# Head outputs of a 32-step linear recurrence with a token on each partition: row sums from the squaring instruction, scaling in the PSUM copy, four transposes back

## The chip, the core and the metric

The kernel runs on one core of one Trainium2 chip. The metric is the time of one execution in device microseconds (us); lower is better. Five engines matter: TensorE (PE in the profile; its weight loads are PEld), VectorE (DVE), ScalarE (ACT), GpSimd (POOL) and SyncE (SP), whose queue issues the weight transfers. Each engine takes its instructions strictly in the order in which they were written to its queue.

## The reference, cut to what matters

Two networks run one after the other on 512 tokens of width 1024. The change lies in the HGRN2 mixer near the end. It has 8 heads of 128 channels, works on chunks of 32 tokens, and normalizes each head's output for each token over the head's 128 channels:

```python
    o = o_intra + jnp.moveaxis(o_inter, 0, 2)
    o = o.transpose(0, 2, 3, 1, 4).reshape(B, S, H, DV)
    gate = jax.nn.silu(g_x.astype(jnp.float32)).reshape(B, S, H, DV)
    o = rms_norm(o, o_norm) * gate
    return o.reshape(B, S, HV).astype(h.dtype) @ w_o
```

where `rms_norm(x, g)` is `x * rsqrt(mean(x*x, axis=-1) + 1e-6) * g`.

## The kernel before

Activations lie channel-major: a tile of [128 channels, 512 tokens] for each block of 128 channels. Every large product runs as three products of parts (`mm3`: high by high, high by low, low by high), so an output block with 1024 inputs is 24 TensorE instructions of 128x512. A weight is loaded by SP into `raw`, its high part `wh` is made by ScalarE (line 140) and its low part `wl` by VectorE (line 123).

The mixer is the method `hgrn` (from line 1526). For head `hd` it runs `gates(hd + 1)` (two products, and the elementwise work on `A`, `Q`, `C`, `D`, `E`, `x` for the next head), `states(hd)` (the score products `sc`, the masked scores `hg_AT`, the turned keys `kv`/`kd`, the block states `st`), `out_gates(hd)` (the product whose gate is the tile `G`) and `outputs(hd)` (from line 1697), which is what changes. `vt` holds the values of all heads with a token on each partition. After the last head come the products with `w_o`: three output blocks (`mm`) that wait for the last heads' outputs, then blocks of half the tokens (`sm`).

The program's text isn't the order on the engines: a scheduler with its own model of times fixes, when the kernel is built, one order for each engine. So a changed instruction can move others. The order is fixed then, and an engine whose next instruction isn't ready stands still.

In PSUM, `hgrn` has two banks for `mm`, three for `sc`, one for `kv` and two for `po`. The tag `po` serves the head's output product and, before the change, two more tiles for each head: the sums over the channels (`tokstat`) and the factors spread over the partitions (`bcast`). Their products are these lines of the two helpers, and the factor itself is made by `rstd` (a small VectorE instruction at line 130 and a power on POOL at line 245):

```python
self.mm(ps[:, i * nb + tb : i * nb + tb + 1], a[:, s.start + tb * P : s.start + (tb + 1) * P], self.ones[:, 0:1])
...
self.mm(ps[:, o : o + P], c[:, tb : tb + 1].to_broadcast([P, P]), self.ident)
...
self.ts(out, sums, 1.0 / n, EPS)
self.pow_(out, out, -0.5)
```

In `outputs` before the change, the channels of the head lie on the partitions. ScalarE copies `po` (to the tile tagged `B`) and squares it (to `C`); TensorE sums the squares over the partitions (`po<-ones,C`), `rstd` gives `wo`, TensorE spreads it (`po<-ident,wo`), VectorE multiplies twice (line 133), and the result is split into `aH` (ScalarE) and `aL` (VectorE) for the products with `w_o`.

Of the kernel before, what the change touches and what calls it, by code (L numbers as in the profile page):

```python
# [20 lines left out]
P = 128  # L21
T = 512
# [26 lines left out]
class Acts:  # L49
    """Channel-major activations split exactly into two float32r parts."""  # L50
# [11 lines left out]
class Kern:  # L62
# [18 lines left out]
    def wpool(self, parts):  # L81
        """room for so many more split weights, taken in turns"""
        self.wx.append(ExitStack())
        pool = self.wx[-1].enter_context(self.pool(self.name("wp"), parts, side="left"))
        self.wslots.append([pool] * parts)

    def wclose(self):
        """takes back what was given last"""
        self.wx.pop().close()
        self.wslots.pop()  # L90
        self.wn = 0

    def psums(self, tags, keep=0):
        """PSUM banks, so many for each tag; the first pools may stay"""
# [16 lines left out]
    @contextmanager  # L111
    def ordered(self):
        """each engine issues the elementwise instructions within in the order of the program"""
        old, self.token = self.token, self.name("order")
        yield
        self.token = old
# [40 lines left out]
    def wload(self, src, k, m, eng=None):  # L157
        """src: DRAM [k*128, m] -> raw tile view [128, k, m]"""
# [31 lines left out]
    def gemm(self, w, col0, acts, K, evac, idx, m=P, leng=None, tag="mm"):  # L190
        """one chunk of m output channels: psum[m, T] = w[:, col0:col0+m].T @ acts"""
# [9 lines left out]
    def gemm_halves(self, w, cols, acts, K, evac, idxs, then=None, tags=None):  # L201
        """chunks of output channels, the first half of the tokens of all of them before the second"""
# [10 lines left out]
    def split(self, src, hi, lo, g=None):  # L213
        """hi + lo = src * g, exactly split; src fp32 in SBUF"""
# [8 lines left out]
    def tokstat(self, acc_list, s=FULL, tag="sm"):  # L223
        """acc tiles [128, T] -> psum [128 tok, len * blocks] of the sums over partitions"""
# [7 lines left out]
    def bcast(self, *cols, tag="sm"):  # L232
        """[128 tok, blocks] each -> psum [128, blocks * 128] each, the same on every partition"""
# [43 lines left out]
    def params(self, tag, rows_tile):  # L277
        """parameters, channel on partition: their loads and what turns them"""
# [22 lines left out]
    def block1(self):  # L301
# [10 lines left out]
        mod = self.cp.tile([P, 24], F32, tag="mod", name="mod")  # shift, 1 + scale, gate  # L312
# [6 lines left out]
        # what the output projection and its norm need again waits in DRAM  # L319
# [21 lines left out]
        def ada_load(pool, k, lo, n, bufs):  # L341
            """n blocks of w_ada, lo * 8 + k, (lo + 1) * 8 + k, .."""
# [6 lines left out]
        def ada_acc(acc, raw, steps=range(9)):  # L349
            """silu(c)'s products with them, but for the sum over partitions; two sums in turns"""  # L350
# [27 lines left out]
        # shift and scale of a chunk of channels are summed while the chunk before is modulated  # L378
        def modulated(k, xt, acc):
            """shift and scale, x turned and modulated"""  # L380
# [50 lines left out]
        def shift_evac(ps, mc, out, v3=False):  # L431
            """out = p + mu * (p one token before - p)"""
# [8 lines left out]
        # -------- masks  # L441
        mk2 = b([P, 2, RC], "mk2")  # columns t of A (s < t) and of R (s <= t); rows s twice
# [5 lines left out]
        # rows (head, s), columns (head, t): s in the lower, t in the upper half of one head  # L448
# [6 lines left out]
        # -------- B branch: low-rank inputs of decay and in-context rate  # L455
# [8 lines left out]
        hp = b_([P, 16], "hp")  # w0/2, a0/2, k_a/2, 1-k_a/2  # L464
# [22 lines left out]
        def prep(p):  # L487
            """what a pair of heads brings to the windows, in parts that other products may come between"""
# [52 lines left out]
        def lmat(p, hf):  # L541
            """for half of the windows of a pair: products of all of B | K with all of A | R, masked"""
# [14 lines left out]
        # -------- A branch: norm of v, mixing over the tokens of a block  # L557
# [56 lines left out]
        # -------- products that nothing waits for: they fill the tensor engine between the others  # L614
# [9 lines left out]
        def v_part(p):  # L624
            """values, and the bonus of the current token"""
# [5 lines left out]
        # gate of the B branch: (gn * g + b + bonus) * silu(gate) = gn * G2 + B2  # L631
# [43 lines left out]
        def fill(n):  # L675
            """so many steps of what fills"""
# [13 lines left out]
        def a_free():  # L690
            """the windows' products take the A branch's place"""
# [4 lines left out]
            # of the first four windows where the residual will be  # L696
# [45 lines left out]
        def inverse():  # L742
            """inverses of the 32x32 diagonal blocks of I - L, one block per partition"""
# [29 lines left out]
        def merge(c):  # L773
            """inverses of the 64x64 blocks, transposed"""
# [36 lines left out]
        def chain(c, between):  # L811
            """one window; what else there is comes between its dependent products"""
# [4 lines left out]
            # one accumulation group per bank: the first product alone clears it  # L817
# [38 lines left out]
        def post(tb):  # L856
            """group norm over a head's channels, bonus, gate"""
# [27 lines left out]
        def out_gate(k):  # L885
            """gate of the output, one chunk"""
# [39 lines left out]
        def between(c, late):  # L926
            """the next window's inputs, and the norm of what is complete"""
# [56 lines left out]
        # -------- output projection, residual, layer norm  # L984
# [10 lines left out]
        def o_evac(n, i, ps, s):  # L995
# [5 lines left out]
            else:  # L1001
                self.tt(a1, a1, y, ALU.add)
                sq = (s1, s2)[n % 2][:, HALVES[s.start == 0]]  # the half that holds no sums now
# [3 lines left out]
        # the weight stays for the second half of the tokens, some of it where the attention's inputs will be  # L1007
# [59 lines left out]
    # chunk k of acts = res * gain, split  # L1067
# [7 lines left out]
    def sumsq(self, acc, y, k, pool, s, tag="sq"):  # L1075
        """acc[:, s] += y ** 2, the first for k = 0"""
# [12 lines left out]
    def rstd(self, out, sums, n, fac=None):  # L1089
        """out = (sums / n * fac + EPS) ** -0.5 for [128 tok, NB] columns"""  # L1090
# [7 lines left out]
    def norms(self, m, s2, g, w, s, pre, r2=None):  # L1098
        """res += m * rms(m) * gain; with r2 the true m is m * r2 per token;
        pre: the next norm's acts, gain, sums of squares and a pool"""  # L1100
# [32 lines left out]
    def gemm_tail(self, w, acts, K, evac, norm, begun=()):  # L1133
        """eight chunks; the last four by halves of the tokens, norm(s) after each"""
# [17 lines left out]
    def mla(self):  # L1152
        nc, I, tc = self.nc, self.I, self.tc
        if True:
# [8 lines left out]
            # -------- the products start before the first norm's per-token factor is known  # L1163
# [8 lines left out]
            def c_evac(i, ps, s):  # L1172
# [4 lines left out]
                else:  # split when the factor per token is there  # L1177
# [6 lines left out]
            # rotary key: its columns twice, so that both halves of the partitions hold it  # L1184
# [9 lines left out]
            # -------- rotation tables: cos, and sin with the sign of the row's half  # L1194
# [50 lines left out]
            # the queries' factor enters with the scale of the scores  # L1245
# [27 lines left out]
            # -------- values, token-major  # L1273
# [17 lines left out]
            # -------- attention  # L1291
            oa = self.new_acts()

            def scores(q, qr, k, qb):
                """softmax of the query block's scores, [128 queries, keys]"""
# [48 lines left out]
            def project_q(hp, tags=("mm", "mm")):  # L1344
# [11 lines left out]
                # one head each: its upper parts on its half of the partitions, the lower ones on the other  # L1356
# [37 lines left out]
    def mixer_out(self, nm, w_o, o, gpost, gpre, begun=()):  # L1394
        """res += rms(o @ w_o); the MLP's normed input"""
# [130 lines left out]
    def hgrn(self):  # L1526
# [3 lines left out]
        with ExitStack() as ox:  # L1530
            oa = self.new_acts()
            with ExitStack() as mx:
# [164 lines left out]
                def outputs(hd, AT, st, E, G):  # L1697
                    hs = slice(hd * P, (hd + 1) * P)
                    po = self.ptl("po")
                    for tb in range(NB):  # L1700
                        s = slice(tb * P, (tb + 1) * P)
                        self.mm(po[:, s], vt[tb][:, hs], AT[:, tb, :], start=True, stop=(tb == 0))
                        if tb:
                            self.mm(po[:, s], st[:, tb, :], E[:, s], start=False, stop=True)
# [72 lines left out]
```

## Time and profile before

| | before |
|---|---|
| median of three runs | 1627.69 us (1627.19 to 1629.02) |
| span of the profiled execution | 1623.7 us |
| TensorE busy, share of the span | 1554.1 us, 96% |
| VectorE busy | 947.0 us, 58% |
| ScalarE busy | 704.4 us, 43% |
| POOL busy | 325.0 us, 20% |
| transfers, mean | 100 GB/s |

The span runs from the first to the last instruction of the profiled execution. No time of its own is given for that execution beside the span; the median of the runs lies 4.0 us above the span, and that is what lies around it. The mixer's heads run from about 1026 to 1221.5 us of the span.

### The profile page before, as it was taken

To read this page: it belongs to the slowest core of one execution; us is meant where nothing else is said; L and a number is where in the kernel's file an instruction comes from. 1 tells how busy PE (TensorE), PEld (TensorE's weight loads), DVE (VectorE), ACT (ScalarE), POOL (GpSimd) and SP (SyncE) were. 2 spreads that over 40 slices of the span, in tenths; PEclk is the share of its full clock that TensorE was granted. 3 is DMA by queue.
4 is the path that set the end of the run, shared out by engine and by line. 5 is a ranking of instruction groups with operands and counts; after the bars stand their busy time and mean duration, and the time that the engine had idled before them with its cause. 6 is when DMAs were issued, how large, how long until landed. Compare 5 with 4: busy or idle time off the path is not lost. (4 is left out here: it accounts for less than half of the span.)

```text
span 1623.7 us, 22045 instructions
## 1 busy us (share of the span) xinstructions
PE 1554.1 (96%) x8389; PEld 1317.7 (81%) x8389; DVE 947.0 (58%) x1651; ACT 704.4 (43%) x1217; POOL 325.0 (20%) x459
## 2 busy tenths in 40 slices
PE   5987979999999999999999999999999999999998
PEld 4766768889978899888888887888889988888886
DVE  7798595678667738233343456677754824343445
ACT  3533315655666645332232334666535523322331
POOL 4465631234310023000000032222313200000000
PEclk9998889999999999999999999999999999999999
DMA  9732445544123133333333232322213223231421
GB/s 290 219 96 82 75 130 144 176 139 112 52 69 91 33 111 90 93 92 102 91 93 102 80 102 66 103 66 66 71 47 105 91 79 115 64 120 65 120 88 52
DMA packets 272894, 161.70 MB, mean 100 GB/s; under 512 B 29465, under 2 KB 253316, under 8 KB 272788
## 3 DMA queue, kind: packets, MB, share of 16 engines
q1 hardware_dynamic: 271492, 157.33, 33.6%
q0 software_dynamic: 1152, 2.70, 0.5%
q8 instruction: 66, 1.08, 0.3%
q14 instruction: 40, 0.33, 0.1%
q10 hardware_dynamic: 144, 0.26, 0.1%
HBM read 147.42 MB, written 11.53 MB: 98 GB/s over the span
## 5 line engine op out<-in xcount | busy, mean ns | idle before, releaser
L123 DVE TENSOR_TENSOR wl<-raw,wh 128x1024 fp32r<-128x1024 f32 (+2 forms) x228 | 272.1, 1194 | 291.1 <-ACT wh L140 287.0
L140 ACT CAST wh<-raw 128x1024 fp32r<-128x1024 f32 (+3 forms) x244 | 242.6, 996 | 449.1 <-PE mm L143 354.2
L143 PE MATMUL mm<-bL,wh 128*128 128x512 f32 (+1 forms) x752 | 282.6, 378 | 1.0 <-DVE bL L133 1.0
L143 PE MATMUL mm<-bH,wl 128*128 128x512 f32 (+1 forms) x752 | 281.5, 377 | 0.0
L143 PE MATMUL mm<-bH,wh 128*128 128x512 f32 (+1 forms) x752 | 278.9, 378 | 0.1
L143 PE MATMUL mm<-aH,wh 128*128 128x512 f32 (+1 forms) x656 | 240.6, 369 | 11.2 <-DVE gt L133 7.0
L143 PE MATMUL mm<-aH,wl 128*128 128x512 f32 (+1 forms) x656 | 236.8, 362 | 1.5 <-DVE wl L123 1.5
L143 PE MATMUL mm<-aL,wh 128*128 128x512 f32 (+1 forms) x656 | 237.7, 363 | 0.0
L143 PEld LDWEIGHTS mm<-bL,wh 128*128 128x128 f32 x752 | 141.1, 188 | 29.0 <-DVE bL L133 1.8
L143 PEld LDWEIGHTS mm<-bH,wl 128*128 128x128 f32 x752 | 141.1, 188 | 27.4
L143 PEld LDWEIGHTS mm<-bH,wh 128*128 128x128 f32 x752 | 139.1, 188 | 28.4 <-ACT hg_vt L137 0.5
L143 PEld LDWEIGHTS mm<-aH,wh 128*128 128x128 f32 x656 | 125.1, 191 | 33.4 <-DVE gt L133 7.9
L143 PEld LDWEIGHTS mm<-aH,wl 128*128 128x128 f32 x656 | 125.1, 191 | 20.7 <-DVE wl L123 1.9
L143 PEld LDWEIGHTS mm<-aL,wh 128*128 128x128 f32 x656 | 125.5, 191 | 18.3 <-issue 0.7
L143 PE MATMUL mm<-wh,aH 128*128 128x512 f32 x288 | 113.5, 396 | 1.5 <-ACT aH L140 1.5
L143 PE MATMUL mm<-wh,aL 128*128 128x512 f32 x288 | 112.6, 393 | 0.0
L143 PE MATMUL mm<-wl,aH 128*128 128x512 f32 x288 | 112.5, 392 | 0.0
L140 ACT CAST aH<-t 128x512 fp32r<-128x512 f32 (+1 forms) x74 | 41.1, 564 | 75.7 <-DVE t L123 75.5
L123 POOL TENSOR_TENSOR mlpt<-mlpt,sq 128x256 f32<-128x256 f32 (+1 forms) x9 | 11.9, 1320 | 306.5 <-ACT sq L137 306.5
L245 POOL TENSOR_TENSOR mlpss<-mlpss,pwm 128x1 f32<-128x1 f32 x4 | 2.2, 547 | 321.8 <-DVE mlpss L128 321.8
L123 DVE TENSOR_TENSOR aL<-t,aH 128x512 fp32r<-128x512 f32 (+1 forms) x74 | 45.0, 617 | 36.2 <-ACT aH L140 36.2
L143 PEld LDWEIGHTS mm<-wh,aH 128*128 128x128 f32 x288 | 54.6, 190 | 12.8 <-ACT aH L140 1.9
(546 smaller groups left out, 2831.4 us busy)
## 6 DMA issues: line engine op xcount, KB each, us to landing
raw<-in_mlp_w_dram SPq DMA_DIRECT2D x128, 512.0 KB
raw<-in_hgrn_w_in_dram SPq DMA_DIRECT2D x32, 512.0 KB
raw<-in_w_in_dram SPq DMA_DIRECT2D x23, 512.0 KB
ada<-in_w_ada_dram SPq DMA_DIRECT2D x16, 512.0 KB
raw<-in_w_out_dram SPq DMA_DIRECT2D x10, 512.0 KB
raw<-in_w_ada_dram SPq DMA_DIRECT2D x8, 512.0 KB
raw<-in_mla_w_o_dram SPq DMA_DIRECT2D x8, 512.0 KB
raw<-in_hgrn_w_o_dram SPq DMA_DIRECT2D x8, 512.0 KB
```

Source lines behind the costliest of these rows:

```text
L123: self.st((eng or self.nc.vector).tensor_tensor(out=out, in0=a, in1=b, op=op))
L140: self.st(self.nc.scalar.copy(out=out, in_=in_))
L143: i = self.nc.tensor.matmul(out, l, r, start=start, stop=stop, **kw)
L245: self.nc.gpsimd.tensor_tensor(out=out, in0=a, in1=cst[: a.shape[0], :n], op=ALU.pow)
```

## The change

Both products of `outputs` have their operands swapped, so that `po` holds the 128 tokens of a block on the partitions and the head's channels along the free axis. A token's sum of squares is then a sum along a row, which each of four squaring instructions of ScalarE leaves in a column of `wo` through its accumulator. `rstd` works on those four columns. ScalarE copies `po` in four pieces, each scaled by its tokens' factor (one value for each partition), TensorE turns each piece back with a transpose (`pt`, from the same `po` banks), and VectorE multiplies the turned tile by the norm's gain (with the half of the gate folded into a new column `hon`, made once) and the gate in one instruction, in place in `G`. The rest of the diff takes out comments and docstrings.

```diff
@@ in hgrn
+                hon = vp.tile([P, 1], F32, tag="hon", name="hg_hon")
+                self.ts(hon, self.pc("on"), 0.5)
...
@@ in outputs
                     for tb in range(NB):
                         s = slice(tb * P, (tb + 1) * P)
-                        self.mm(po[:, s], vt[tb][:, hs], AT[:, tb, :], start=True, stop=(tb == 0))
+                        self.mm(po[:, s], AT[:, tb, :], vt[tb][:, hs], start=True, stop=(tb == 0))
                         if tb:
-                            self.mm(po[:, s], st[:, tb, :], E[:, s], start=False, stop=True)
+                            self.mm(po[:, s], E[:, s], st[:, tb, :], start=False, stop=True)
                     o = self.tl(mp, [P, T], "B")
-                    self.copy(o, po)
                     sq = self.tl(mp, [P, T], "C")
-                    self.act(sq, po, AF.Square)
-                    wo = self.tl(mp, [P, NB], "wo")
-                    self.rstd(wo, self.tokstat([sq], tag="po"), P)
-                    pr = self.bcast(wo, tag="po")
-                    self.stt(o, o, self.pc("on"), pr, ALU.mult, ALU.mult)
-                    self.stt(o, o, 0.5, G, ALU.mult, ALU.mult)
-                    self.split(o, oa[hd][0], oa[hd][1])
+                    wo = self.tl(mp, [P, 2, NB], "wo")
+                    for tb in range(NB):
+                        s = slice(tb * P, (tb + 1) * P)
+                        self.act(sq[:, s], po[:, s], AF.Square, accum=wo[:, 0, tb : tb + 1])
+                    self.rstd(wo[:, 1], wo[:, 0], P)
+                    pt = self.ptl("po")
+                    for tb in range(NB):
+                        s = slice(tb * P, (tb + 1) * P)
+                        self.act(o[:, s], po[:, s], AF.Copy, scale=wo[:, 1, tb : tb + 1])
+                        self.turn(pt[:, s], o[:, s])
+                    self.stt(G, pt, hon, G, ALU.mult, ALU.mult)
+                    self.split(G, oa[hd][0], oa[hd][1])
```

On TensorE, the order changes from the first head's output on, and is the same again from the first `sm` product after the last head. Between two products of 128x512 that belong to one output block, "..." stands for the others of it. First, TensorE where head 3's output (`po_10178` before, `po_10180` after) is done and head 4's scores (`sc`) begin, before the change:

```order
L143 MATMUL po_10178<-E_9877,st_10134 128x128
L143 MATMUL mm_10251<-bL_6257,wh_10247 128x512
...
L143 MATMUL sc_10313<-D_10078,A_10001 128x128 x4
L143 MATMUL sc_10318<-E_10083,x_10097 128x128
L143 MATMUL po_10191<-ones,C_10188 128x1 x4
L143 MATMUL sc_10318<-E_10083,x_10097 128x128 x3
L143 MATMUL sc_10323<-E_1718_10101,K_1719_10102 64x64 x4
L143 MATMUL mm_10355<-bH_6250,wh_10351 128x512
...
L143 MATMUL po_10198<-ident,wo_10190 128x128 x4
L143 MATMUL kv_10334<-ident,x_10097 128x128 x3
```

The same place after the change:

```order
L143 MATMUL po_10180<-st_10136,E_9879 128x128
L143 MATMUL mm_10253<-bH_6260,wl_10250 128x512
...
L143 MATMUL sc_10315<-D_10080,A_10003 128x128 x4
L143 MATMUL sc_10320<-E_10085,x_10099 128x128 x4
L143 MATMUL sc_10325<-E_1715_10103,K_1716_10104 64x64 x4
L143 MATMUL mm_10357<-bH_6250,wh_10353 128x512
...
L149 MATMUL po_10197<-ident,B_10188 128x128
L143 MATMUL mm_10357<-bL_6259,wh_10353 128x512
...
L149 MATMUL po_10197<-ident,B_10188 128x128 x2
```

Before, 14 products stand between the output and the scores, the sums come among the scores, and the spread factors after 23 of the next block's 24 products. After, 7 products stand ahead of the scores, and the transposes come after the 13th, 16th and 17th product of the next block, one, one and two at a time.

Second, TensorE at the last head's output (`po_10896` before, `po_10898` after), before the change:

```order
L143 MATMUL po_10896<-E_10701,st_10852 128x128
L143 MATMUL mm_11075<-aL_8950,wh_11071 128x512
...
L143 MATMUL mm_11075<-aH_8951,wl_11072 128x512
L143 MATMUL po_10909<-ones,C_10906 128x1 x4
L143 MATMUL mm_10931<-aH_8953,wh_10927 128x512
...
L143 MATMUL mm_11075<-aH_8953,wl_11072 128x512
L143 MATMUL po_10916<-ident,wo_10908 128x128 x4
L143 MATMUL sm_11128<-aH_8941,wh_11106 128x256
```

The same place after the change:

```order
L143 MATMUL po_10898<-st_10854,E_10703 128x128
L143 MATMUL mm_10933<-aH_8953,wh_10929 128x512
...
L143 MATMUL mm_11077<-aH_8953,wl_11074 128x512
L149 MATMUL po_10915<-ident,B_10906 128x128 x4
L143 MATMUL sm_11130<-aH_8941,wh_11108 128x256
```

Before, 5 products, the sums, 9 products (the three blocks' inputs from head 6, `aH_8953`) and the spreading stand between the last output and the first `sm` product. After, the 9 products and the transposes stand there, and the 5 products have gone ahead of the output.

Third, ScalarE around head 3's output (`A` is the next head's gate), before the change:

```order
L137 ACT_TABLE_LOAD
L137 ACTIVATE A_10207<-A_10207 128x512
L140 COPY B_10186<-po_10178 128x512
L137 ACTIVATE C_10188<-po_10178 128x512
L137 ACT_TABLE_LOAD
L137 ACTIVATE A_10207<-A_10207 128x512
```

The same place after the change (`C,wo` are the squares with their sums, `B<-po,wo` the scaled copies):

```order
L137 ACT_TABLE_LOAD
L137 ACTIVATE A_10209<-A_10209 128x512
L137 ACTIVATE C_10189,wo_10190<-po_10180 128x128 x4
L140 CAST wh_10624<-raw_10622 128x1024
L137 ACTIVATE Q_10246<-x_10278 128x512
L137 ACTIVATE B_10188<-po_10180,wo_10190 128x128 x4
L137 ACT_TABLE_LOAD
L137 ACTIVATE A_10209<-A_10209 128x512
```

The second table load and the second pass over `A` have moved from right behind the square of `po` to behind the scaled copies, which wait for POOL's power. The number of table loads is the same.

## Rows read from the trace of the kernel before

**Rows 1.** Windows: stretch, its length, each engine's busy time (instructions), granted clock, DMA.

```profile
1026.00:1221.50 195.50, 195.43 (x1106) 166.57 (x1105) 135.97 (x211) 111.15 (x164) 54.16 (x119) 1.00 0.23 65
1221.50:1260.00 38.50, 36.55 (x271) 34.43 (x270) 19.65 (x28) 20.60 (x41) 13.65 (x13) 1.00 0.38 112
```

**Rows 2.** Chain that ended last: start, duration, engine, tile, line, instructions.

```profile
1400.07 200.75 PE mm L143 x874
```

**Rows 3.** Timeline of TensorE after head 0's output: start, duration, what.

```profile
1061.34 1.05 PE L143 MATMUL sc<-D,A 128*128 128x128 f32 x8
...
1063.83 0.50 PE L143 MATMUL mm<-bH,wh 128*128 128x512 f32 x1
...
1064.40 0.95 PE L143 MATMUL po<-ones,C 128*128 128x1 f32 x8
1065.21 0.48 PE L143 MATMUL mm<-bH,wl 128*128 128x512 f32 x1
1065.53 0.39 PE L143 MATMUL mm<-bH,wh 128*128 128x512 f32 x1
...
1072.61 1.05 PE L143 MATMUL po<-ident,wo 128*128 128x128 f32 x8
1073.50 0.61 PE L143 MATMUL po<-hg_AT,hg_vt 128*128 128x128 f32 x4
```

**Rows 4.** Timeline of TensorE, head 0's three transposed key blocks.

```profile
1047.60 0.49 PE L1680 MATMUL kv<-ident,x 128*128 128x128 f32 x3
1047.92 0.61 PE L143 MATMUL po<-hg_AT,hg_vt 128*128 128x128 f32 x4
```

**Rows 5.** Timeline of ScalarE: a 128x128 instruction with its accumulator read.

```profile
474.73 0.46 ACT L137 ACTIVATE P<-sm,st,w 128x128 f32<-128x128 f32 x1
475.09 0.19 ACT L137 ACTIVATION_READ_ACCUMULATOR P<-sm,st,w 128x1 f32 x1
475.18 0.39 ACT L140 CAST wh<-raw 128x256 fp32r<-128x256 f32 x1
```

**Rows 6.** Groups by line and form, ScalarE: busy us, mean ns | idle before.

```profile
L137 ACT ACTIVATE S<-S,PC 128x128 f32<-128x128 f32 x24 | 8.8, 397 | 0.3
...
L140 ACT COPY PT<-pt 128x128 f32<-128x128 f32 x8 | 2.2, 270 | 0.3 <-PE pt L1317 0.2
```

**Rows 7.** Timelines of ScalarE, VectorE and POOL behind the last head's output.

```profile
1216.47 0.59 ACT L140 COPY B<-po 128x512 f32<-128x512 f32 x1 [13.17 <-PE po L143]
...
1218.70 0.16 DVE L130 TENSOR_SCALAR wo<-po 128x4 f32<-128x4 f32 x1
...
1219.01 1.01 POOL L245 TENSOR_TENSOR wo<-wo,pwm 128x4 f32<-128x4 f32 x1 [9.57 <-DVE wo L130]
```

**Rows 8.** Timelines of TensorE, VectorE and POOL after head 1's output.

```profile
1085.96 0.95 PE L143 MATMUL po<-ones,C 128*128 128x1 f32 x8
...
1090.23 0.15 DVE L130 TENSOR_SCALAR wo<-po 128x4 f32<-128x4 f32 x1
...
1090.47 1.39 POOL L245 TENSOR_TENSOR wo<-wo,pwm 128x4 f32<-128x4 f32 x1 [1.24 <-DVE wo L130]
```

**Rows 9.** Timeline of TensorE, from the last head's output on.

```profile
1215.99 0.39 PE L143 MATMUL po<-E,st 128*128 128x128 f32 x2
1216.13 0.47 PE L143 MATMUL mm<-aL,wh 128*128 128x512 f32 x1
...
1217.61 1.05 PE L143 MATMUL po<-ones,C 128*128 128x1 f32 x8
...
1220.69 1.05 PE L143 MATMUL po<-ident,wo 128*128 128x128 f32 x8
1221.50 0.36 PE L143 MATMUL sm<-aH,wh 128*128 128x256 f32 x1
```

**Rows 10.** Windows of 4 us from a pause of TensorE on (columns as in Rows 1).

```profile
116.00:120.00 4.00, 0.97 (x6) 0.97 (x8) 4.00 (x7) 1.15 (x2) 0.20 (x1) 0.84 0.06 18
120.00:124.00 4.00, 4.00 (x26) 3.50 (x25) 2.30 (x6) 0.00 (x0) 1.18 (x1) 0.73 0.49 185
```

## The prediction

> **What bounds the kernel now.** I read the windows first. Over the eight heads (1026 to 1221.5 us) TensorE is busy 195.43 of 195.50 us at the full granted clock, while VectorE has 135.97 and ScalarE 111.15 us of work there [rows 1]; per head that is 24.4 us of TensorE, 17.0 of VectorE, 13.9 of ScalarE. From there to 1260 us TensorE is idle for 2 us, and the chain that ended last is then TensorE alone: 874 instructions in 200.75 us, 0.23 us for a 128x512 product [rows 2]. So a microsecond of TensorE taken out of the heads comes off the end, as long as nothing makes TensorE wait instead. What the other engines gain or lose counts only through such waits.
>
> **TensorE, removed.** I take a block's cost as the time from its start to the next start, since ends overlap. The sums over partitions take 1064.40 to 1065.21, 0.81 us for a head; where they stand ahead of a large product, that product takes 0.32 us instead of 0.23, 0.09 more [rows 3]. Spreading the factors takes 1072.61 to 1073.50, 0.89 us [rows 3]. Both are eight instructions for four blocks: each float32 product is two passes, even the one with a single column.
>
> **TensorE, added.** Four transposes of 128x128. The row for this form is the turned keys: three in 0.32 us, one pass each, so four are 0.43 us [rows 4]. Where they stand ahead of a large product the 0.09 us come on top. By the order, the four stand together ahead of small blocks in heads 0, 1 and 6, ahead of a large product in heads 2 and 4, and in three pieces among large products in heads 3 and 5 (three times 0.09). The swapped products keep their number and shape, 128x128 by 128x128 either way, so I cost them at nothing, and no row gives a reason for another value.
>
> So heads 0 to 6 save 0.81 + 0.89 - 0.43 = 1.27 us in heads 1 and 6, 1.36 in head 0 (whose sums stood among large products), 1.18 in heads 2 and 4, 1.00 in heads 3 and 5: together 1.36 + 2.54 + 2.36 + 2.00 = 8.3 us.
>
> **ScalarE, VectorE, POOL.** A head loses a 512-wide copy and square and gains four 128-wide squares, four accumulator reads and four scaled copies. An instruction of that width with its read takes 474.73 to 475.18, 0.45 us [rows 5]; a copy of 128x128 out of PSUM takes 0.27 us, one with a scale from a tile 0.40 [rows 6]. That is 1.8 + 1.6 us in place of two at about 0.59 [rows 7], so some 16 us of ScalarE in a head of 23 us, still with room. VectorE loses one pass of 512. These hide under TensorE except where TensorE waits for the result.
>
> **Heads 0 to 6, does TensorE wait?** From the last product of an output to the transposes TensorE has this to do in head 3: 7 products (1.6 us), the scores (1061.34 to 1063.83, 2.5 us [rows 3]), 13 products (3.0 us), 7.1 us in all; in the others, by the same count in the order, 6.8 to 8.3. The chain it must cover: squares 1.8, the small VectorE instruction and POOL's power 0.3 + 1.0 to 1.4 [rows 7, 8], copies 1.6, about 5.2 us. That leaves 1.5 us or more, so I take no wait here. If the cover is gone, TensorE stands still with the next head's output products behind it in its queue.
>
> **The last head.** Here little work is left. Before, from the last output (1216.13) to the first `sm` product (1221.50) lie 5.4 us, nearly full of work [rows 9]. After, I put the new chain on the same clock. Squares start at 1216.47, where the copy of `po` starts now [rows 7]; four at 0.45 end at 1218.4. The small instruction follows 0.1 later, the power starts 0.3 after that (as 1218.70 and 1219.01 stand) and takes 1.0 [rows 7], to 1219.8. Four scaled copies at 0.40 end at 1221.4, the last transpose and the `sm` product follow at 1221.6. TensorE has only nine products to fill this with, 2.1 us, then it idles about 2.8 us. So the `sm` products start as late behind the last output as before, though 5 products (1.15 us) have gone ahead of that output. The last head therefore costs 1.15 + 0.1 = 1.25 us instead of saving any.
>
> Bounds for this term: the cheapest rows, 0.27 for each square and copy with free reads [rows 6], bring the end 1.2 us earlier; the dearest, 0.46 + 0.19 for a square with its read in full [rows 5], 0.46 for a copy and 1.39 for the power [rows 8], bring it 1.4 us later. I take the middle because the pair in rows 5 is the same pair of instructions at the same width.
>
> The Trainium skill, page "VectorE: DVE Perf Modes", section on the TRN2 errata, speaks against splitting like this: ScalarE pays a fixed latency with every instruction, and tiles of 512 or more are advised. Its formula for a PSUM source (172 cycles plus the width, at 1.2 GHz) gives 0.25 us at 128, an estimate that agrees with the 0.27 us of rows 6 for a plain copy but has no accumulator read; with it eight instructions are 2.0 us instead of 3.4, and the sum would come to 1619.3 us.
>
> **The sum.** -8.3 + 1.25 = -7.0 us: the span from 1623.7 to 1616.7, and with the 4.0 us around it, from a median of 1627.69 to 1620.7 us. A change of 0.2%, 3.3 us, is about what a measurement of this kernel tells from none.
>
> **Rivals.**
> *The last head loses nothing.* If squares and copies are as cheap as the cheapest rows and no head pays the 0.09 us of a switch, the heads give up to 7 x 1.36 = 9.5 us and the last head costs nothing: about 1618.2. For it speaks that a plain PSUM copy takes 0.27 us; against it, the accumulator's read has its own row.
>
> *The pause costs the clock.* In the window from 116 us TensorE was busy 0.97 of 4 us, and the granted clock was 0.84 there and 0.73 in the next [rows 10]; the level below full is 1.2 GHz instead of 2.4. That loss is 0.16 x 4 + 0.27 x 4 = 1.7 us. The new pause, 2.8 us, is a little shorter. If it does the same, the time is 1622.4. [...]
>
> *The chain is late in every head.* After head 1 the sums start at 1085.96, but the small VectorE instruction that reads them runs at 1090.23, 3.3 us after their end, since VectorE does other instructions ahead of it, and POOL's power then takes 1.39 [rows 8]. After the change this instruction again stands behind other work of VectorE, and ScalarE queues the next head's second table load and pass over the gate behind the scaled copies. With 3.3 us more the chain is about 8.5 us against a cover of 6.8 to 8.3, a wait of some 1 us in each of seven heads: 1620.7 + 7 = 1627.7, no change. From 1.5 us each it is slower by more than the measurement tells, around 1631. Against it: the chain has 1.5 us or more in hand in every head, and head 1's delay didn't make TensorE wait before.
>
> **How the numbers follow.** The forecast, 1620.7, has a chance of 0.50; the larger gain 0.14; the clock's loss 0.18; the late chain 0.18, of which no change 0.10 and slower 0.08. The first three are faster by over 0.2%: 0.82. The range goes from 1617.5, just below the larger gain, to 1625.5, which takes in the bounds of the last head, the clock and a wait of up to 0.7 us a head, and leaves out about 2 in 10. The forecast's own range is 1619.5 to 1622.1, from the bounds of the last head.
>
> **What would show it.** In the changed kernel the heads from 1026 us on should take about 8 us less, with 32 one-pass transposes and no `po<-ones` or `po<-ident,wo`. TensorE should have no wait for `B` in heads 0 to 6, and one of 2 to 3.5 us for the last head's `B`. ScalarE's squares with their reads should stand about 0.45 us apart. The prediction is wrong if TensorE waits for `B` or for the next scores in the middle heads, if ScalarE's small instructions take over 0.65 us, or if the granted clock falls below 1.00 behind the last head.

## The result and the profile after

| | before | after |
|---|---|---|
| median | 1627.44 us (1625.90 to 1629.02, 4 runs) | 1616.88 us (1615.60 to 1619.43, 4 runs) |
| ratio, 95% interval | | 0.9936 [0.9922, 0.9950] |
| span of the profiled execution | 1623.7 us | 1613.8 us (its own time 1615.6 us) |
| head 0's first output product to the first `sm` product | 173.58 us [rows 4, 9] | 163.94 us |

The change makes the kernel 0.64% faster, 10.6 us where I had forecast 7.0, and the median lies 0.6 us under the low end of my range. The page's first part for the changed kernel, each engine's busy time, share of the span and instructions:

```profile
span 1613.8 us, 21901 instructions
PE 1542.8 (96%) x8293; PEld 1305.5 (81%) x8293; DVE 939.0 (58%) x1644; ACT 713.3 (44%) x1297; POOL 329.5 (20%) x459
```

TensorE lost 96 instructions: 64 for the sums, 64 for the spread factors, and 32 transposes came. Windows of the changed kernel (columns as in [rows 1], which they answer):

```profile
1026.00:1213.00 187.00, 186.15 (x1020) 156.56 (x1019) 130.61 (x204) 120.24 (x245) 58.00 (x119) 1.00 0.25 70
1208.00:1212.00 4.00, 3.15 (x16) 2.11 (x15) 0.37 (x2) 2.06 (x12) 1.61 (x2) 1.00 0.10 30
1212.00:1216.00 4.00, 4.00 (x28) 3.69 (x28) 1.24 (x2) 1.26 (x2) 0.00 (x0) 1.00 0.28 101
```

In the heads TensorE is idle for 0.85 us in 187, at the full granted clock, and the second row says where: behind the last head's output. The clock is 1.00 there and in the window behind. TensorE's waits of the changed kernel from 1020 to 1240 us (what waits for what: us in total, times, longest):

```profile
PE po L149 <- ACT B L137: 0.9, 1, 0.9
PE mm L143 <- ACT hgms L137: 0.5, 1, 0.5
```

So no transpose of heads 0 to 6 waits; the one wait for `B` is the last head's. (The wait for `hgms`, in the norm behind the heads, stands in the kernel before as well, with the same 0.5 us.) Groups by line and form of the changed kernel, 1026 to 1214 us (columns as in [rows 6]):

```profile
L245 POOL TENSOR_TENSOR wo<-wo,pwm 128x4 f32<-128x4 f32 x8 | 10.2, 1275 | 55.2 <-DVE wo L130 55.2
L137 ACT ACTIVATE B<-po,wo 128x128 f32<-128x128 f32 x32 | 9.1, 367 | 5.4 <-POOL wo L245 5.4
L137 ACT ACTIVATE C<-po 128x128 f32<-128x128 f32 x32 | 8.4, 278 | 15.4 <-PE po L143 15.4
L137 ACT ACTIVATION_READ_ACCUMULATOR C<-po 128x1 f32 x32 | 6.6, 207 | 0.0
```

A square's mean is 0.28 us and a read's 0.21, but they overlap. The timeline of ScalarE behind the last head's output shows how far apart they stand (start, duration, what):

```profile
1207.77 0.28 ACT L137 ACTIVATE C<-po 128x128 f32<-128x128 f32 x1 [1.84 <-PE po L143]
1207.94 0.19 ACT L137 ACTIVATION_READ_ACCUMULATOR C<-po 128x1 f32 x1
1208.04 0.27 ACT L137 ACTIVATE C<-po 128x128 f32<-128x128 f32 x1
...
1210.23 1.14 ACT L137 ACTIVATE B<-po,wo 128x128 f32<-128x128 f32 x4 [1.32 <-POOL wo L245]
```

From square to square it is 0.27 and then 0.25 us, read included, and four scaled copies take 1.14, 0.29 each. [Rows 5] had given 0.45 and [rows 6] 0.40. TensorE at the same place, which answers to [rows 9]:

```profile
1207.35 0.39 PE L143 MATMUL po<-st,E 128*128 128x128 f32 x2
1207.49 0.94 PE L143 MATMUL mm<-aH,wh 128*128 128x512 f32 x3
...
1210.66 1.10 PE L149 MATMUL po<-ident,B 128*128 128x128 f32 x4 [0.85 <-ACT B L137]
1211.52 0.36 PE L143 MATMUL sm<-aH,wh 128*128 128x256 f32 x1
```

**Where the time came from.** From the first large product behind the last output to the first `sm` product it is 1207.49 to 1211.52, 4.03 us, against 1216.13 to 1221.50, 5.37 us [rows 9]. Five products, 1.15 us, have gone ahead of that output, so the last head gains 1.34 - 1.15 = 0.19 us. From head 0's output to that large product it was 168.21 us and is 159.91, with the five products more: heads 0 to 6 give 8.30 + 1.15 = 9.45 us, 1.35 each. Together 9.64; the span fell by 9.9, since the heads began 0.3 us sooner. Behind the first `sm` product nothing changed: from its start to the end of the span it is 402.2 us before and 402.3 after.

Granted clock and start of the heads differ from one execution to the next, by some us that have nothing to do with the change (in every run the same 5456 TensorE instructions stand ahead of head 0's output): in the runs below head 0's output stands anywhere from 1047.6 to 1054.4 us. So I compare the stretch from head 0's first output product to the first `sm` product (173.58 before, 163.94 after), in which the granted clock was 1.00 but for the pauses told of below, and give the medians beside it.

### The profile page after: what moved, and what is told of

The parts are those of the page before. It is cut to its first block, busy times and chain, and to the rows that moved or that the text cites. A ratio compares the mean times of both kernels' runs of the same rounds, so it can differ in the third digit from the quotient of the medians.

```text
span 1613.8 us, 21901 instructions
## 1 busy us (share of the span) xinstructions
PE 1542.8 (96%) x8293; PEld 1305.5 (81%) x8293; DVE 939.0 (58%) x1644; ACT 713.3 (44%) x1297; POOL 329.5 (20%) x459
```

## The experiments

My theory after the result: every head's two float32 blocks cost 0.89 us each on TensorE and the transposes 0.43, in whichever order; ScalarE's chain costs only where TensorE has nothing else, in the last head, and there it is shorter than I had it. Rivals: that the gain comes from something else than the two blocks (the swapped products, ScalarE's or VectorE's lighter work), and that the prediction's 1.25 us for the last head was right and the heads gave still more.

### The sums over partitions again

```diff
                     for tb in range(NB):
                         s = slice(tb * P, (tb + 1) * P)
+                        self.mm(pt[:, tb : tb + 1], sq[:, s], self.ones[:, 0:1])
+                    for tb in range(NB):
+                        s = slice(tb * P, (tb + 1) * P)
                         self.act(o[:, s], po[:, s], AF.Copy, scale=wo[:, 1, tb : tb + 1])
```

> The changed kernel, but TensorE again sums the squares of each head with four one-column products, into the bank that the transposes overwrite; the sums are thrown away. I compare the stretch from head 0's first output product to the first half-width product behind the last head: 173.6 us before, 163.9 after the change. Theory (the gain is TensorE work taken out of a full engine): the block costs 0.89 us a head, 8 heads give 7.1, so the stretch is 171.0 and the time about 1624. Rival (the gain comes from the shorter chain or from the new order, and TensorE's small blocks are hidden): the stretch stays at 164 to 165 and the time at 1617.

Measured: stretch 1054.39 to 1223.94, 169.55 us, 5.6 more than after; median 1623.97 us, ratio to before 0.9981 [0.9970, 0.9991]. That is nearer to the theory's 171.0 than to the rival's 164 to 165, and 1.5 short. TensorE behind the last output in this kernel:

```profile
1216.75 0.39 PE L143 MATMUL po<-st,E 128*128 128x128 f32 x2
...
1221.77 0.95 PE L143 MATMUL po<-ones,C 128*128 128x1 f32 x8
...
1223.35 0.49 PE L149 MATMUL po<-ident,B 128*128 128x128 f32 x3
```

From 1216.89 to 1221.77, 4.9 us, stand large products; TensorE has no wait here. The scheduler put 21 products between the last output and the sums, 25 in all behind that output, where the changed kernel has nine, and the changed kernel's wait is gone. What hiding that wait is worth by itself the last part of this section measures: 1.4 us, a stretch of 162.57 us. Against that stretch the sums take 6.98 us, 0.87 a head, and the 1.5 us that were missing from the theory's 171.0 are the hidden wait. The sums cost what they cost before, and the wait can be hidden.

### Each block turned twice

```diff
                         self.turn(pt[:, s], o[:, s])
+                        self.turn(pt[:, s], o[:, s])
```

> The changed kernel with each transpose of a head's output issued twice, 32 more transposes. Theory (TensorE work): 0.43 us a head, 3.4 in all, stretch 167.4, time about 1620.3. If a block of transposes also pays the 0.09 us switch that the prediction charged, up to 0.7 more. Rival (hidden): stretch 163.9.

Measured: stretch 1050.90 to 1217.39, 166.49 us, 2.55 more; median 1620.06 us, ratio 0.9956 [0.9941, 0.9971]. Here too the scheduler hid the wait, with 21 products behind the last output. Against the 162.57 us without a wait the second transposes take 3.92 us, 0.49 a head where the theory has 0.43. TensorE's eight in head 0, and in head 3:

```profile
1073.32 1.03 PE L149 MATMUL po<-ident,B 128*128 128x128 f32 x8
1074.19 0.61 PE L143 MATMUL po<-hg_vt,hg_AT 128*128 128x128 f32 x4
...
1134.89 1.09 PE L149 MATMUL po<-ident,B 128*128 128x128 f32 x8
1135.91 0.56 PE L143 MATMUL sc<-E,K 128*64 128x64 f32 x6
```

In head 0 it is 0.87 us for eight, 0.11 each. In head 3 the order of this kernel puts them among the 64x64 products (`sc<-E,K`), and there they take 1.02 us, so a part of the 0.06 a head is the place where they stand. In the changed kernel they cost that one by one too; head 3's:

```profile
1133.76 0.27 PE L149 MATMUL po<-ident,B 128*128 128x128 f32 x1
...
1134.56 0.27 PE L149 MATMUL po<-ident,B 128*128 128x128 f32 x1
...
1134.90 0.38 PE L149 MATMUL po<-ident,B 128*128 128x128 f32 x2
```

From 1133.76 to 1134.56 are one transpose and three products: 0.80 - 3 x 0.23 = 0.11. The 0.09 us that I had added per piece isn't there.

### Only the last head in its old form, only the last head in its new one

`outputs_ch` is the function of before, with a channel on each partition.

```diff
-                    outputs(hd, *z, out_gates(hd))
+                    (outputs if hd < 7 else outputs_ch)(hd, *z, out_gates(hd))
```

> Heads 0 to 6 as changed, head 7 in the old form (channels on the partitions, sums and factors through TensorE). The prediction's own step says that the new form costs 1.25 us at the last head, so undoing it there would give a stretch of 162.7. Theory from the trace after (squares with their reads 0.25 us apart, not 0.45): the new form costs nothing there; the old chain behind the order's nine products (2.1 us), sums 0.9, factor 1.6, spread 0.8 makes 5.4 us against 4.0, so the stretch is 165.3.

```diff
+                    (outputs if hd == 7 else outputs_ch)(hd, *z, out_gates(hd))
```

> Heads 0 to 6 in the old form, head 7 as changed. Theory from the trace after: the old order leaves 14 products behind the last output, 3.3 us, which cover the new chain of 3.2 us, so the last head saves the whole 1.35 us: stretch 172.2, time about 1626. The prediction's step (the last head loses 1.25): stretch 174.8, time about 1628.7.

Measured: with the last head old, stretch 165.28 us (1048.29 to 1213.57), 1.34 more than after; median 1618.92, ratio 0.9950 [0.9936, 0.9965]. With it alone new, 172.96 us (1048.46 to 1221.42), 0.62 less than before; median 1626.65, ratio 0.9999 [0.9990, 1.0009]. Both sides say that the last head in its new form gains, 0.6 to 1.3 us by what the scheduler puts around it, where the prediction had it losing 1.25 (162.7 and 174.8 us). The first stretch is the theory's to 0.1 us; the second misses the theory's 172.2 by 0.8. (The 162.7 and 174.8 charge the form with the 1.15 us of five products gone ahead of the output, an order that neither kernel undoes. Without it the prediction's step would give 163.8 and 173.7, and both measured stretches miss these on the same side.) The waits show why the two sides differ; with the last head old, and with it alone new:

```profile
PE po L143 <- POOL wo L245: 1.3, 1, 1.3
```

```profile
PE po L149 <- ACT B L137: 0.2, 1, 0.2
```

The old form waits as well, for the power, when nine large products stand behind the output (with 14, in the kernel before, it did not wait for the power). The new form behind 14 products should by the theory have waited for nothing. But where the heads ahead are old, ScalarE has a cast of head 6 between the first square and the second:

```profile
1217.07 0.28 ACT L137 ACTIVATE C<-po 128x128 f32<-128x128 f32 x1 [13.22 <-PE po L143]
...
1217.34 0.61 ACT L140 CAST aH<-B 128x512 fp32r<-128x512 f32 x1
1217.84 0.28 ACT L137 ACTIVATE C<-po 128x128 f32<-128x128 f32 x1
```

The second square comes 0.77 us behind the first instead of 0.27. So the chain outlasts the 14 products, and the transposes go at the pace of the copies, 0.86 us for the four (1220.56 to 1221.42).

### All squares twice

```diff
                         self.act(sq[:, s], po[:, s], AF.Square, accum=wo[:, 0, tb : tb + 1])
+                        self.act(sq[:, s], po[:, s], AF.Square, accum=wo[:, 0, tb : tb + 1])
```

> The changed kernel with every square and its accumulator read issued twice in all eight heads (the results are the same): ScalarE has 4 x 0.25 = 1.0 us more to do between each head's output and its scaled copies. This scheduler order puts no product behind the last head's output, so the last head's chain stands bare. Theory (heads 0 to 6 had over 2.5 us in hand, since the chain measured 4.0 us against 6.8 to 8.3 us of other products): no wait of TensorE for B in heads 0 to 6; one pause for the last B of 3.3 + 1.0 - 0.1 = 4.2 us instead of 0.85; the stretch from head 0's output to the first sm product 163.9 - 0.85 + 4.2 = 167.3 us, the time about 1620.3. The late-chain rival of the prediction (heads 0 to 6 just hide the chain, so 1.0 us more shows in each): 7 x 1.0 more, a stretch of 174, about 1627. If the pause costs the clock: granted clock under 1.00 in the windows behind it and 1.7 us more behind the stretch.

Measured: stretch 1048.74 to 1216.37, 167.63 us; median 1622.91, ratio 0.9975 [0.9964, 0.9986]. TensorE's wait for `B`:

```profile
PE po L149 <- ACT B L137: 4.5, 1, 4.5
```

One wait, in the last head, and none in the seven others. But the scheduler's order is another here: from an output's last product to its first transpose TensorE has 9.2 to 11.4 us in heads 0 to 6, where the changed kernel has 6.8 to 9.6, so this run by itself doesn't show what reserve the changed kernel had. That kernel's own trace does. In head 6, which has the least:

```profile
1199.70 1.15 ACT L137 ACTIVATE B<-po,wo 128x128 f32<-128x128 f32 x4 [0.95 <-POOL wo L245]
...
1203.73 0.60 PE L149 MATMUL po<-ident,B 128*128 128x128 f32 x4
```

The copies are done at 1200.85, 2.9 us ahead of the first transpose; in the other six heads it is 3.0 to 3.4 us. A chain late by 1.0 us more would still have been hidden: the late chain is refuted. The pause of this run is 0.3 us longer than expected: the four repeats took 1.6 us and not 1.0, since a square repeated into the same place stands 0.40 us behind the first (next part), and the rest of the sum was 0.3 us too long. What I hadn't expected is TensorE's clock. Windows of this kernel:

```profile
1213.00:1214.00 1.00, 0.00 (x0) 0.00 (x0) 0.17 (x1) 0.69 (x5) 0.00 (x0) 1.00 0.00 0
1214.00:1215.00 1.00, 0.00 (x0) 0.00 (x0) 0.00 (x0) 0.00 (x0) 0.99 (x2) 0.50 0.00 0
...
1219.00:1220.00 1.00, 1.00 (x7) 1.00 (x6) 0.00 (x0) 0.00 (x0) 0.00 (x0) 0.50 0.00 0
```

TensorE stops at 1210.95, the granted clock falls from 1.00 to 0.50 (from 2.4 to 1.2 GHz) before TensorE starts again at 1215.47, and stays there behind the pause.

### A longer pause in the last head alone

```diff
-                        self.act(sq[:, s], po[:, s], AF.Square, accum=wo[:, 0, tb : tb + 1])
+                        for _ in range(4 if hd == 7 else 1):
+                            self.act(sq[:, s], po[:, s], AF.Square, accum=wo[:, 0, tb : tb + 1])
```

> The changed kernel with the last head's squares issued four times (results the same): its chain is 12 x 0.25 = 3.0 us longer, all of it a pause of TensorE behind the last head's output, 0.85 + 3.0 = 3.85 us; the other heads are as they were. Theory (a pause costs its own length and nothing more): stretch 163.9 + 3.0 = 166.9 us, granted clock 1.00 in the windows behind it, time about 1619.9. Rival from the prediction (such a pause costs the clock): granted clock of about 0.73 to 0.84 in a window of 4 to 8 us behind the pause and 1.7 us more there, about 1621.6. If it is shorter than 3.85 us by a constant, the squares repeat faster than 0.25 us.

Measured: stretch 1048.74 to 1217.50, 168.76 us; median 1624.17, ratio 0.9981 [0.9972, 0.9991]. The pause is 5.64 us, not 3.85. ScalarE's timeline, the first and second square of one block, and the first of the next:

```profile
1208.92 0.28 ACT L137 ACTIVATE C<-po 128x128 f32<-128x128 f32 x1 [1.85 <-PE po L143]
...
1209.32 0.28 ACT L137 ACTIVATE C<-po 128x128 f32<-128x128 f32 x1
...
1210.38 0.27 ACT L137 ACTIVATE C<-po 128x128 f32<-128x128 f32 x1
```

Twelve repeats at 0.40 are 4.8 us, and 0.85 + 4.8 = 5.65. The granted clock fell here too, while TensorE stood still (until 1216.60), so the pause costs more than its length:

```profile
1214.00:1215.00 1.00, 0.00 (x0) 0.00 (x0) 0.11 (x1) 0.79 (x5) 0.00 (x0) 0.50 0.00 0
```

The same with two squares instead of four puts the pause near the 2.8 us that the prediction had:

```diff
-                        for _ in range(4 if hd == 7 else 1):
+                        for _ in range(2 if hd == 7 else 1):
```

> The changed kernel with the last head's squares issued twice (results the same). In the run with all squares twice four more squares took 1.62 us more, so the pause is 0.85 + 1.62 = 2.47 us, near the 2.8 us that the prediction had for the changed kernel. If a pause of this length does not cost the clock, the granted clock stays 1.00 and the stretch is 163.94 + 1.62 = 165.6 us; if it does, as behind the pauses of 4.52 and 5.64 us, the sm products behind it stand 0.21 us apart instead of 0.12 for some 3.4 us and 1.7 us more are lost behind the stretch.

Measured: pause 2.45 us, stretch 1048.44 to 1214.00, 165.56 us, as worked out; median 1618.75, ratio 0.9947 [0.9932, 0.9962]. Its windows and TensorE's rows:

```profile
1212.00:1213.00 1.00, 0.00 (x0) 0.00 (x0) 0.00 (x0) 0.32 (x2) 1.00 (x2) 0.91 0.00 0
...
1212.00:1216.00 4.00, 2.90 (x13) 2.67 (x14) 0.93 (x2) 1.76 (x5) 1.25 (x2) 0.60 0.35 131
```

```profile
1213.10 1.25 PE L149 MATMUL po<-ident,B 128*128 128x128 f32 x4 [2.45 <-ACT B L137]
1214.00 0.56 PE L143 MATMUL sm<-aH,wh 128*128 128x256 f32 x1
1214.36 0.41 PE L143 MATMUL sm<-aL,wh 128*128 128x256 f32 x1
...
1216.27 0.28 PE L143 MATMUL sm<-aL,wh 128*128 128x256 f32 x1
1216.38 0.28 PE L143 MATMUL sm<-aH,wl 128*128 128x256 f32 x1
```

The clock falls in this pause as well, before TensorE starts again at 1213.10: the `sm` products stand 0.21 us apart until 1216.3, then 0.12. Eleven of them take 2.38 us; at 0.12 they are 1.4 (in the kernel of the next part, 1212.35 to 1213.74), so 1.0 us is lost, not the 1.7 that I expected. Behind 0.85 us in the changed kernel nothing is lost. The way from the first `sm` product to the end of the span says the same: 403.3 us here, 402.3 in the changed kernel. Behind the pauses of 4.52 and 5.64 us it is 404.1 and 403.2 us, so 1.8 and 0.9 us are lost there: in these three the clock's price doesn't grow with the pause. The span, 1617.3 us beside 1615.0 for the changed kernel on the same chip, carries both, 2.3 us for 1.6 + 1.0 (its heads began 0.4 us sooner); the medians of four and five runs, 1618.75 and 1618.01, are too scattered to show it.

### Products moved behind the last output

The last head's output products and the last four of the eight channel steps of one output-projection chunk are kept in program order on TensorE:

```diff
+                    self.petoken = "tail" if hd == 7 else None
                     for tb in range(NB):
                         s = slice(tb * P, (tb + 1) * P)
...
+                    self.petoken = None
...
+            if self.late:
+                self.petoken = "tail" if k >= 4 else None
             self.mm3(ps[:m], wh[:, k, :], wl[:, k, :], acts.hi(k), acts.lo(k), k == 0, k == K - 1)
...
+            self.late = begun and i == 3
             self.gemm(w, i * P, acts, K, evac, i)
```

> The changed kernel with six products of an output-projection chunk moved from ahead of the last head's output to behind it, 15 products instead of 9 there, so that they cover the chain; nothing else differs on TensorE. Theory (the 0.85 us is a wait for the last scaled copy, 3.3 us behind the last output, and 15 x 0.23 = 3.4 us cover it): no wait for B, stretch 163.94 - 0.85 = 163.1 us, time about 1616.0 with a ratio to the kernel before 0.0005 below the changed kernel's. Rival: the state products of the last head, now sooner behind the state's VectorE instructions, wait for these instead; then a wait for st of up to 0.85 us shows and the stretch stays at 163.9.

> The kernel with six products behind the last head's output once more, on the same chip as the changed kernel. If its shorter stretch (162.57 against 163.94 us) reaches the end, its median is 1.2 to 1.5 us below that of the changed kernel; if the later norms or the weights' transfers take it back, the two are alike within 0.3 us.

Beside the second ran the changed kernel itself:

> The changed kernel itself once more, beside the next one on the same chip. Stretch from head 0's output to the first sm product 163.9 us, pause 0.85 us, time 1616 to 1618.

Measured, in the first run: stretch 1049.78 to 1212.35, 162.57 us, no wait for `B` and none for the state; median 1614.19, ratio 0.9922 [0.9909, 0.9936]. In the second, 1050.30 to 1212.85, 162.55 us; median 1616.26 (1614.11 to 1616.89), ratio 0.9931 [0.9918, 0.9943]. The changed kernel beside it has 163.92 us, a median of 1618.01 (1616.83 to 1620.76) and 0.9945 [0.9933, 0.9958]. TensorE in the first:

```profile
1208.17 0.39 PE L144 MATMUL po<-st,E 128*128 128x128 f32 x2
...
1211.85 0.74 PE L150 MATMUL po<-ident,B 128*128 128x128 f32 x4
1212.35 0.37 PE L144 MATMUL sm<-aH,wh 128*128 128x256 f32 x1
```

Fifteen products now stand between, and the transposes find nearly all of `B` ready: they take 0.50 us to the `sm` product where they took 0.86, paced by the copies. That is 0.36 us; and the wait, 0.85 us of idle time, is 1.0 us by the starts (the product ahead of it starts at 1209.41, and 0.23 later the transposes could have). That is why the stretch gains 1.4 us and not 0.85. Both medians are the lowest of their chips, and the medians on one chip differ by 1.75 us, somewhat more than the expected 1.2 to 1.5; the intervals of the two ratios still overlap, so the total time alone only suggests the gain. The traces show that it reaches the end: from the first `sm` product to the end of the span it is 402.2 to 402.3 us in both runs of this kernel as in both of the changed one.

## Why the prediction was right in direction and short in size

- **What bounds the kernel: right.** TensorE is idle 0.85 of 187 us in the heads, and what its two blocks cost came off the end. The lighter work of ScalarE and VectorE had nothing to give in heads 0 to 6, where TensorE waited for neither before the change.
- **TensorE removed and added, "together 8.3 us": mis-sized.** It measured 9.45. I had given the sums 0.81 us and the 0.09 behind them only ahead of a large product; the block behind pays some 0.08 in every head, whatever it is, so they are 0.89. Head 2's, ahead of small products, before the change:

```profile
1110.56 0.95 PE L143 MATMUL po<-ones,C 128*128 128x1 f32 x8
1111.43 0.68 PE L143 MATMUL sc<-E,K 128*64 128x64 f32 x8
```

And I had charged the transposes 0.09 for each piece among large products; a single one costs 0.11 us and no more, by the rows of head 3 and by the doubled transposes. 0.89 + 0.89 - 0.43 = 1.35 in all seven heads. The run with the sums put back, 0.87 a head, agrees. No run put the spread factors back alone; their 0.89 rests on the rows and on the 9.45 that they make up with the rest. The run with only the last head new, which has both blocks in heads 0 to 6, gives that sum again: 168.27 us to the first large product behind the last output (1048.46 to 1216.73) against 159.91, and the five products, 9.5 in all. That the swapped products cost nothing was right. One pair of them before and after, whose next pairs start at 1215.99 [rows 9] and 1207.35:

```profile
1215.77 0.39 PE L143 MATMUL po<-hg_AT,hg_vt 128*128 128x128 f32 x2
...
1207.12 0.39 PE L143 MATMUL po<-hg_vt,hg_AT 128*128 128x128 f32 x2
```

It is 0.22 and 0.23 us for two, 0.11 each either way.
- **"Heads 0 to 6, does TensorE wait?": right.** No wait, and the copies were done 2.9 us or more ahead of the transposes. The rival of a late chain falls.
- **"The last head therefore costs 1.25 us": the step that failed.** It gains 0.19. The chain is 1.2 us shorter: four squares with reads took 1.1 us instead of 1.9, four copies 1.14 instead of 1.6, while the small instruction and the power came as forecast. I took 0.45 from [rows 5] as the same pair of instructions at the same width. It isn't: that one is an exponential whose bias and scale come from tiles (`st`, `w`); these are squares with constants, though both read PSUM. The bound that I had worked out from the cheapest rows, 0.27 each with free reads, was the better row for every instruction. Nearer rows for the square stood in the trace before, squares of PSUM with constants:

```profile
L137 ACT ACTIVATE C<-po 128x512 f32<-128x512 f32 x8 | 4.8, 604 | 0.0
...
L137 ACT ACTIVATE sq<-mm 128x256 f32<-128x256 f32 x12 | 4.7, 389 | 0.0
```

By the step from 512 to 256 elements a square of 128 takes 0.28 us, an estimate that the measured 0.28 meets. What makes [rows 5] dearer no run took apart. The lengths at 128 elements out of PSUM, 0.28 us with constants, 0.37 with the scale from a tile (the scaled copies) and 0.46 with scale and bias from tiles, speak for the operands; but the functions differ as well.
- **The Trainium skill, page "VectorE: DVE Perf Modes", section on the TRN2 errata,** gave 0.25 us for each of these, an estimate without the read. The measured 0.25 to 0.27 from square to square agrees with it, read included. Its advice against small tiles is right about ScalarE's load (713.3 us of it in the span instead of 704.4) and made no difference to the time in the seven heads where TensorE hid it.
- **"The pause costs the clock": a true mechanism, below its point here.** The changed kernel's pause is 0.85 us and the clock stayed at 1.00. Had it been the 2.8 us of my sum, the clock would have fallen, as behind 2.45 us. So my likeliest case was not consistent with itself: it held the pause and not its price, some 1.0 us. The Trainium skill, page "TensorE: Matmul & The Clock Gate", section "Why this matters for your kernels", warns against idle gaps in the middle of a kernel. That such a gap costs the clock the run with the 2.45 us pause shows too (0.60 in its window); but the gap that the page names is longer than this one, and the measurement decides.
- **"The 4.0 us around the span": off.** The changed kernel's profiled execution took 1615.6 us for a span of 1613.8, 1.8 us around it. In the other runs it is 1.7 to 2.1. The 4.0 had set one execution's span against the median of others. It stands on both sides of the sum, so the forecast gain of 7.0 us doesn't hang on it.

The rival "the last head loses nothing", 1618.2 us, was the nearest, and for the reasons that it names: 9.5 us from the heads and nothing lost behind them. Against the 7.0 us forecast for the span, the heads give 1.15 more, the last head 1.44, and the start of the heads 0.3, which is 9.9. The median's 10.6 is 0.7 more, within what runs of one kernel differ: when the changed kernel ran again, its median of 1618.01 us was 8.9 us below the 1626.89 of the kernel before beside it, with the same stretch (163.92). So that the first median fell below the range's low end of 1617.5 us, and the second above it, is chance; that the gain is 9.6 us in the stretch and not 7.0 is not, and the two terms named above are the reason.

## What to carry to other kernels

Size a new instruction's cost from rows that share its function and operands as well as its width: a square with constants and its read stood 0.25 us from the next, an exponential with tiles for bias and scale 0.45. Where a short chain moves off the busiest engine, count what that engine still has to do behind the chain's start: seven heads hid it at no cost, the eighth waited, and six products moved behind its start hid that too. A pause of the busy engine has two prices, its length and, beyond some length, the clock behind it (nothing at 0.85 us, 1.0 us more at 2.45, 1.8 at 4.52 and 0.9 at 5.64).

## What the runs showed of the hardware

- An accumulator read of 0.19 to 0.22 us adds little to its square: from square to square it is 0.25 to 0.27 us, a plain copy's length. A second square into the same place as the one before starts 0.40 us behind it instead.
- Transposes of 128x128 cost 0.11 us each, in a block of eight as singly among large products; eight among 64x64 products took 1.02 us.
- Four float32 products with a single output column take eight TensorE instructions and, with what the block behind pays, 0.89 us, as much as four with 128 columns (0.89 us).
- The clock fell to 0.50 while TensorE stood still, before its next instruction, behind pauses of 2.45, 4.52 and 5.64 us; it stayed there for some us of full work (to 1216.3 behind a restart at 1213.10).
